# Weight parts of the first layer and of the experts at other distances from their activations, modulo 256 bytes

## The chip, the cores and the metric

One core of one Trainium2 chip runs the whole program. The time is that of the device, in microseconds; lower is better. The kernel before was timed at 2464.36 us, the median of two runs (2462.41 and 2466.32).

## The reference, cut to what matters

A two-layer transformer-like block (256 image tokens, 256 context tokens, width 1024) and then a second block on the image tokens, all in float32.

```python
for layer in range(2):
    p_lat = h_lat @ w_in[layer]            # q, kv, hyena v/x/y, gates
    ...                                    # attention and a long convolution
    mix = (g_attn * (o_attn @ w_br_attn) + g_hy * (o_hy @ w_br_hy)) @ w_out
    x = x + g1 * mix
    if layer == 0: x = x + g2 * swiglu(h)  # dense feed-forward, 2816 hidden; the context tokens too
    else:          x = x + g2 * moe_swiglu(h)   # 8 experts of 2816 hidden, the two best of each token
x = rmsnorm(x, final_g)
# second block: feed-forward, mixer, feed-forward, each between norms
```

Nearly all of the time is matrix products with weights that are read once: 574 MB come from HBM.

## The kernel before, in words

**One weight tile.** Weights lie in HBM as tiles of 128 partitions by up to 1024 columns. `wraw` (line 525) loads one by DMA from the SP queue into a buffer `raw`. `whl` (line 540) splits it into two parts of type fp32r whose sum is the weight: ScalarE copies it rounded to `whi` (`split`, line 502), VectorE writes the rest to `wlo`. `mm3` (line 497) then makes each product from three matmuls, weight high by activation high, weight high by activation low, weight low by activation high, and the line of all matmuls in the profile is that of the helper `mm`, L495. A tile of eight 128-column chunks so gives 24 matmuls. Every matmul loads its own stationary operand of 128 columns, and the load for the next matmul runs beside the present one.

**Who is stationary.** In layer 0, layer 1 and block 2 the weight chunk is stationary and the activations move: 512 columns (image and context tokens together) in layer 0 and for keys and values, 256 in layer 1 and block 2. In the experts (`moe`) and for `v2` the activations (`xe`, `hm`, `h`) are stationary and the weights move, 512 columns at a time, 256 in the last of an expert's six groups of hidden columns (`g == 5`) and for `v2`.

**Where tiles lie.** Tiles come from pools, each a stretch of bytes in every partition, laid out one behind another: first `w` (four `whi` and four `wlo`), then `r` (four `raw`); in the first two layers `b1` (13 general tiles of 8192 bytes: `h`, `fh`, `mg`, `o`, `oh`) and `k1` (work tiles); in the experts `r2`, `k2`, `t2`; in block 2 `b3` and `k3` behind the pool `x2` of the tiles `xsh` and `xsl`. Each `whi` and `wlo` is `self.wc` = 1024 columns of 4 bytes, so all start at a multiple of 256 bytes, and so do their chunks of 512 bytes. The activations of layers 0 and 1 (`h`, `fh`, `mg`, `o`, `oh`) and of the experts (`xe`, `hm`) start at multiples of 256 too. In block 2 the two tiles of `x2` are 8256 and 8320 bytes long (`XPAD` = 16 columns), together 192 more than a multiple of 256, so all of `b3` starts at 192.

In what follows the distance of a matmul is the address of the stationary operand that is loaded next, less the address of the moving operand, modulo 256 bytes. It is 0 in layer 0, in layer 1 and in the experts; it is 64 in block 2, where weights at 0 meet activations at 192, and 192 for `v2`, where the roles are swapped.

**Order.** The tile framework orders ScalarE, VectorE and TensorE by priority; SP and POOL run in program order. The order of the instructions does not follow from addresses.

**Normalisation.** `SumSq.rsqrt` (line 360) computes a reciprocal root with a Newton step. It uses a work tile `nm` (one buffer of `self.kn` columns: 512 in the first two layers and the experts, 256 in block 2), beside `nr`, and the squares lie in a ring of four buffers `a`.

Of the kernel before, what the change touches and what calls it, by code (L numbers as in the profile page):

```python
# [9 lines left out]
F32R = mybir.dt.float32r  # L10
# [315 lines left out]
class SumSq:  # L326
# [33 lines left out]
    def rsqrt(self, out=None):  # L360

        p, N, nf = self.p, self.N, self.nf
        if self.acc is not None:
            self.add(self.acc, True)
        n = self.ss.shape[1]
        m = p.wk("nm", n, 1)
        r = p.wk("nr", n, 1)
        p.act(r, self.ss, AF.Abs_reciprocal_sqrt, scale=1.0 / nf, bias=p.epsc if self.eps == EPS else p.eps2)
        p.stt(m, r, -0.5 / nf, r, OP.mult, OP.mult)
        p.stt(m, self.ss, self.eps * nf, m, OP.add, OP.mult)  # L370
        out = r if out is None else out
        p.stt(out, m, 1.5, r, OP.add, OP.mult)
        return out
# [91 lines left out]
class Prog:  # L465
# [53 lines left out]
    def ring(self, name, n, dt, i):  # L519
# [2 lines left out]
        pool = self.rp2 if k >= 4 else self.wp if i else self.rp  # L522
        return pool.tile([128, n], dt, name=name, tag=f"{name}{k}", bufs=1)

    def wraw(self, key, c=slice(None)):
        src = self.wsrc(key)[0][:, c]
        n = src.shape[1]
        raw = self.ring("raw", 1024, F32, 0)
        self.dma(raw[:, :n], src)
        return raw[:, :n]  # L530
# [4 lines left out]

    def w(self, key, k, **kw):

        return self.whl(self.wraw(key), k, **kw)

    def whl(self, raw, k, bufs=None, beside=False):  # L540
        n = raw.shape[1]
        c = n // k
        per = max(1, min(k, self.wc // c))
        r = []
        for s in range(0, k, per):
            m = min(per, k - s)
            if bufs:
                hi, lo = bufs[0]
                bufs.append(bufs.pop(0))
            else:  # L550
                hi, lo = self.ring("whi", self.wc, F32R, 1), self.ring("wlo", self.wc, F32R, 2)
                self.wpairs = (self.wpairs + [(hi, lo)])[-4:]
            with ExitStack() as es:
                es.enter_context(self.tc.high_priority(offset=self.early))
                for ins in self.hold:
                    es.enter_context(self.tc.issue_after(ins))
                if beside:
                    self.act(hi[:, :n], raw)
                    h3, r3 = (t[:, :n].rearrange("p (k c) -> p k c", c=128) for t in (hi, raw))
                    self.tt(h3[:, :, 96:], r3[:, :, 96:], h3[:, :, 64:96].bitcast(F32), OP.subtract)  # L560
                else:
                    self.split(hi[:, :m * c], lo[:, :m * c], raw[:, s * c:(s + m) * c])
            r += [(hi[:, i * c:(i + 1) * c], lo[:, i * c:(i + 1) * c]) for i in range(m)]
        return r
# [84 lines left out]
    def build(self):  # L649
        nc, tc = self.nc, self.tc  # L650
        with ExitStack() as es:
            es.enter_context(tc.manual_schedule(engines={SP, POOL}))
            self.cp = es.enter_context(tc.tile_pool(name="cp", bufs=1))
            self.ps = es.enter_context(tc.tile_pool(name="ps", bufs=1, space=PSUM))
            self.dp = es.enter_context(tc.tile_pool(name="dp", bufs=1, space=DRAM))
            cp = self.cp
            self.cv = cp.tile([128, CTOTAL], F32, name="cv")
            self.ident = cp.tile([128, 128], F32, name="ident")
            self.ones = cp.tile([128, 128], F32, name="ones")

            few = cp.tile([128, 8], F32, name="few")
            self.epsc, self.eps2, self.small, self.tneg = (few[:, i:j] for i, j in ((0, 1), (1, 2), (2, 3), (3, 5)))
            self.gp = cp.tile([128, 6, 8], F32, name="gp")
            self.sp = cp.tile([128, 8], F32, name="sp")
            self.mod = [cp.tile([128, 2, 48], F32, name=f"mod{l}") for l in range(2)]
            self.ada = cp.tile([128, 72], F32, name="ada")
            self.gn = cp.tile([128, 16, 8], F32, name="gn")
            self.xt = cp.tile([128, 8, 512], F32, name="xt")
            self.x = [self.xt[:, k, :] for k in range(8)]
            self.xl = [self.xt[:, k, :NT] for k in range(8)]  # L670
            self.kspill = [self.dp.tile([128, 2048], F32, name=f"ksp{l}") for l in range(2)]
            self.route = cp.tile([128, 10], F32, name="router")
            self.frn = cp.tile([128, 2, 8], F32, name="frn")

            self.rs = cp.tile([128, 8, 2, 8], F32, name="route")
            self.cnt = cp.tile([1, 1], I32, name="cnt")
            self.spill = [self.dp.tile([128, 2048], F32, name=f"sp{i}") for i in range(3)]
            nc.vector.memset(self.ones, 1.0)
            nc.vector.memset(self.epsc, EPS)
            self.fga = cp.tile([128, 2, 8], F32, name="fga")  # L680
            nc.vector.memset(self.eps2, EPS * EPS)
            nc.vector.memset(self.small, 1e-26)
            self.kn, self.early = 512, EARLY[0]
            self.wc, self.turn, self.wbufs, self.wpairs = 1024, [0, 0, 0], [4, 4, 4], []
            self.hold = ()
            c1 = es.enter_context(tc.tile_pool(name="c1", bufs=1))
            self.rope = c1.tile([128, 2, NT], F32, name="rope")
            self.mcst = c1.tile([128, 128 + 256 + 64 + 64], F32, name="mcst")
            with ExitStack() as s0:
                self.wp, self.rp = (s0.enter_context(tc.tile_pool(name=n, bufs=1)) for n in ("w", "r"))  # L690
                with ExitStack() as s1:
                    self.bp = s1.enter_context(tc.tile_pool(name="b1", bufs=13))
                    self.kp = s1.enter_context(tc.tile_pool(name="k1", bufs=1))
                    self.startup()
                    self.layer0()
                    self.layer1()
                self.xsp = s0.enter_context(tc.tile_pool(name="x2", bufs=1, reuse_waits="tile"))
                self.latter("")

            with tc.If(self.most > 128), ExitStack() as s0:  # L700
                self.wp, self.rp, self.xsp = (s0.enter_context(tc.tile_pool(name=n, bufs=1)) for n in ("wg", "rg", "xg"))
                self.latter("g")
# [717 lines left out]
    def moe(self, tp, general):  # L1420
        nc, kp, tc = self.nc, self.kp, self.tc
        m = self.mod[1]
        x = self.xl
# [12 lines left out]
        raws, lows = [], []  # L1436

        def fetch():
            if order:
                key, s, k = order.pop(0)  # L1440
                raws.append((self.wraw(key, s), k))

        def use(key, s, k):
            return ready.pop(0)
# [1 line left out]
        def used():  # L1446

            if raws:
                with self.tc.high_priority(offset=0 if order or len(raws) > 4 else -LATER2):
                    ready.append(self.whl(*raws.pop(0)))  # L1450
                lows.append(self.lo_ins)
                fetch()
        for _ in range(MRAW - 1):
# [162 lines left out]
        def again():  # L1616

            raw = kp.tile([128, 4, 1024], F32, name="xraw", tag="xe", bufs=2)
            turn, bufs = [0], [(self.ring("whi", 1024, F32R, 1), self.ring("wlo", 1024, F32R, 2)) for _ in range(4)]

            def use2(key, s, k):
                turn[0] = (turn[0] + 1) % 4
                t = raw[:, turn[0], :]
                self.dma(t, self.wsrc(key)[0][:, s])
                return self.whl(t, k, bufs)
            self.dma(self.xt[:, :, :NT], self.spill[0].rearrange("p (a b) -> p a b", a=8))
            for i in range(2):
                self.dma(raw[:, 2 * i:2 * i + 2, :], self.spill[1 + i].rearrange("p (a b) -> p a b", a=2))
                self.act(ht[i], raw[:, 2 * i:2 * i + 2, :])
            S = xe = None  # L1630
            for base in (128, 0):
                for e in range(NE):
                    if e % 2 == 0:
                        S = onehot(base, e // 2, S)
                        ST = weights(e // 2, S)
                        xe = gather(e // 2, S, xe)
                    y = expert(e, xe, use2, lambda: None)
                    if base or e < 7:
                        scatter(e, y, ST)
            return (7, y, ST), lambda: [use2((nm, 1, i), slice(0, 1024), 8) for i in range(2) for nm in "gu"]  # L1640
# [342 lines left out]
```

## Time and profile before

| | us |
|---|---|
| median of the two runs | 2464.36 |
| the profiled execution, as timed | 2460.6 |
| its span, first to last instruction | 2458.1 |
| TensorE busy in it | 2400.1 |
| VectorE busy | 1991.8 |
| ScalarE busy | 1500.0 |
| mean granted TensorE clock, share of the full 2.4 GHz | 0.990 |

The profile is of one execution. PE is TensorE's matmuls, PEld its loads of stationary operands, which overlap the matmuls; DVE is VectorE, ACT ScalarE. The bars of matmuls overlap one another, so PE is busy even where a matmul could start sooner. Addresses are not in the trace; the distances above follow from the layout of the pools.

### The profile page before, as it was taken

What the parts mean: (1) busy time and instruction counts of PE and PEld (TensorE: products, weight loads), DVE (VectorE), ACT (ScalarE), POOL (GpSimd) and SP (SyncE); (2) the same over time, 40 slices, a digit from 0 to 9 for tenths busy, and PEclk for the clock granted to TensorE, in tenths of its full rate; (3) what the DMA queues carried; (4) which work ended last, traced back from release to release, by engine and by line L of the source; (5) the groups of instructions that cost most, each with busy time, mean ns of one, the idle gap of its engine ahead of it and who ended that gap; (6) DMA issues with size and microseconds to landing.
All of it is one profiled execution on the core that took longest, in us unless ns stands there. A gap on an engine that the chain in (4) does not pass through costs nothing. (4 is left out here: it accounts for less than half of the span.)

```text
span 2458.1 us, 37467 instructions
## 1 busy us (share of the span) xinstructions
PE 2400.1 (98%) x13896; PEld 2054.5 (84%) x13896; DVE 1991.8 (81%) x3001; ACT 1500.0 (61%) x2214; POOL 89.6 (4%) x170
## 2 busy tenths in 40 slices
PE   8999999999999899999999999999999999999997
PEld 4677887788888698988888888888889998998997
DVE  6787799896878877789988998998987578977655
ACT  6676324422224676687777777777776558767544
POOL 0000011211121000000000000000000000000000
PEclk9999999999999999999999999999999999999999
DMA  7122365687886243699999999999984563454553
GB/s 287 49 92 88 137 230 223 236 293 271 281 312 223 83 140 126 205 382 350 343 351 353 352 339 365 352 332 355 357 298 152 191 220 121 155 176 164 192 194 113
DMA packets 161247, 582.71 MB, mean 237 GB/s; under 512 B 18000, under 2 KB 19536, under 8 KB 159904
## 3 DMA queue, kind: packets, MB, share of 16 engines
q1 hardware_dynamic: 136912, 491.35, 56.1%
q0 software_dynamic: 23600, 88.35, 9.8%
q8 instruction: 111, 1.82, 0.3%
q14 instruction: 80, 0.66, 0.1%
q10 hardware_dynamic: 544, 0.52, 0.1%
HBM read 573.87 MB, written 6.29 MB: 236 GB/s over the span
## 5 line engine op out<-in xcount | busy, mean ns | idle before, releaser
L481 ACT ACTIVATE whi<-raw 128x1024 fp32r<-128x1024 f32 (+1 forms) x902 | 918.2, 1046 | 600.1 <-PE acc L495 376.7
L484 DVE TENSOR_TENSOR wlo<-raw,whi 128x1024 fp32r<-128x1024 f32 (+1 forms) x900 | 1063.8, 1207 | 231.3 <-ACT whi L481 223.2
L495 PE MATMUL acc<-h,whi 128*128 128x256 f32 (+1 forms) x3648 | 829.4, 321 | 9.6 <-ACT h L481 4.6
L495 PEld LDWEIGHTS acc<-h,whi 128*128 128x128 f32 x3648 | 606.2, 189 | 68.2 <-ACT h L481 6.3
L495 PE MATMUL acc<-h,wlo 128*128 128x256 f32 (+1 forms) x1808 | 577.6, 320 | 1.1 <-DVE wlo L484 1.1
L495 PE MATMUL acc<-whi,xe 128*128 128x512 f32 (+1 forms) x1536 | 451.0, 373 | 0.3 <-ACT whi L481 0.3
L495 PEld LDWEIGHTS acc<-h,wlo 128*128 128x128 f32 x1808 | 342.1, 189 | 26.8 <-DVE wlo L484 1.5
L495 PEld LDWEIGHTS acc<-whi,xe 128*128 128x128 f32 x1536 | 280.9, 189 | 48.2 <-ACT whi L481 0.8
L495 PE MATMUL acc<-wlo,xe 128*128 128x512 f32 (+1 forms) x768 | 289.3, 377 | 0.2
L492 DVE SCALAR_TENSOR_TENSOR junk<-wt,rows 128x1024 bf16<-128x1024 f32 x200 | 238.8, 1220 | 4.2 <-DMA wt<-in_w 3.1
L495 PE MATMUL acc<-fh,whi 128*128 128x256 f32 (+1 forms) x1056 | 230.3, 315 | 0.7 <-DVE fh L484 0.6
L495 PE MATMUL y<-whi,hm 128*128 128x512 f32 x704 | 228.5, 395 | 0.0
L495 PEld LDWEIGHTS acc<-fh,whi 128*128 128x128 f32 x1056 | 172.5, 188 | 15.2 <-DVE fh L484 1.5
L495 PEld LDWEIGHTS acc<-wlo,xe 128*128 128x128 f32 x768 | 144.7, 188 | 30.5 <-DVE wlo L484 6.1
L495 PE MATMUL acc<-fh,wlo 128*128 128x256 f32 (+1 forms) x528 | 165.6, 314 | 0.5 <-DVE wlo L484 0.5
L495 PEld LDWEIGHTS y<-whi,hm 128*128 128x128 f32 x704 | 131.3, 188 | 27.4 <-ACT hm L481 3.1
L495 PE MATMUL y<-wlo,hm 128*128 128x512 f32 x352 | 138.5, 397 | 0.6
L495 PEld LDWEIGHTS acc<-fh,wlo 128*128 128x128 f32 x528 | 99.2, 188 | 7.6 <-DVE wlo L484 0.7
L636 POOL DMA_DIRECT2D wt<-in_w x152 | 81.4, 540 | 343.8 <-DVE junk L492 300.0
L495 PE MATMUL acc<-mg,whi 128*128 128x256 f32 (+1 forms) x384 | 86.7, 319 | 0.9 <-DVE mg L484 0.9
L495 PEld LDWEIGHTS y<-wlo,hm 128*128 128x128 f32 x352 | 66.1, 188 | 18.4 <-DVE wlo L484 3.6
L481 ACT ACTIVATE hm<-tp 128x512 fp32r<-128x512 f32 (+1 forms) x48 | 26.9, 561 | 75.0 <-PE tp L1561 74.9
(373 smaller groups left out, 2746.7 us busy)
## 6 DMA issues: line engine op xcount, KB each, us to landing
raw<-in_w SPq DMA_DIRECT2D x890, 512.0 KB, 5.5
wt<-in_w POOLq DMA_DIRECT2D x152, 512.0 KB, 5.7
raw<-in_w SPq DMA_DIRECT2D x24, 384.0 KB, 3.1
xt<-in_x SPq DMA_DIRECT2D x4, 512.0 KB, 9.8
ksp<-hf POOLq DMA_DIRECT2D x2, 1024.0 KB, 5.5
kf<-ksp SPq DMA_DIRECT2D x2, 1024.0 KB, 5.1
sp<-ht POOLq DMA_DIRECT2D x2, 1024.0 KB, 10.3
raw<-in_w SPq DMA_DIRECT2D x8, 256.0 KB, 2.7
```

What stands on the lines that cost most here:

```text
L481: return self.nc.scalar.activation(out, in_, func, **kw)
L484: return self.nc.vector.tensor_tensor(out, a, b, op=op)
L492: return self.nc.vector.scalar_tensor_tensor(out, a, s, b, op0=op0, op1=op1, **kw)
L495: return self.nc.tensor.matmul(out, lhsT=lhsT, rhs=rhs, start=start, stop=stop)
L636: self.nc.gpsimd.dma_start(t[:, i, :], self.wsrc(key)[0])
```

## The change

`whi` and `wlo` become 64 columns (256 bytes) wider, and a weight part is written `off` columns into its tile. `shift(key)` says how far by the kind of the weight:

- layer 1's `q`, `v`, `x`, `y`, `ga`, `gh`, `br`, `wo`, `ukq`: 16 columns, distance 64;
- layer 0's `q`, `v`, `x`, `y`, `ga`, `gh`, `br`, `wo`, `kv`: 40 columns, distance 160;
- layer 0's feed-forward `g`, `u`, `d`: 24 columns, distance 96;
- the experts' gate and up `mg`, `mu`: 32 columns, distance 128 (the weights move here), and 48 in the last group, distance 64;
- the experts' down `md`: 8 columns, distance 224;
- block 2's `v2`: 32 columns, distance 64;
- all others (block 2's other weights, `uv`, `rope`, layer 0's `ukq`, layer 1's `kv`): 0, as before.

The 2048 bytes that the eight wider tiles take are found by `rsqrt`, which takes one of the `a` buffers in place of `nm` where `self.kn` is 512. The list `wpairs`, which nothing read, goes.

```diff
--- before.py
+++ after.py
@@ -363,7 +363,7 @@
         if self.acc is not None:
             self.add(self.acc, True)
         n = self.ss.shape[1]
-        m = p.wk("nm", n, 1)
+        m = p.wk("a", n, 4) if p.kn == 512 else p.wk("nm", n, 1)
         r = p.wk("nr", n, 1)
         p.act(r, self.ss, AF.Abs_reciprocal_sqrt, scale=1.0 / nf, bias=p.epsc if self.eps == EPS else p.eps2)
         p.stt(m, r, -0.5 / nf, r, OP.mult, OP.mult)
@@ -522,6 +522,21 @@
         pool = self.rp2 if k >= 4 else self.wp if i else self.rp
         return pool.tile([128, n], dt, name=name, tag=f"{name}{k}", bufs=1)
 
+    def shift(self, key):
+
+
+        if key[0] in ("q", "v", "x", "y", "ga", "gh", "br", "wo", "ukq") and key[1] == 1:
+            return 16
+        if key[0] in ("mg", "mu"):
+            return 48 if key[2] == 5 else 32
+        if key[0] == "md":
+            return 8
+        if key[0] in ("q", "v", "x", "y", "ga", "gh", "br", "wo", "kv") and key[1] == 0:
+            return 40
+        if key[0] in ("g", "u", "d") and key[1] == 0:
+            return 24
+        return 32 if key[0] == "v2" else 0
+
     def wraw(self, key, c=slice(None)):
         src = self.wsrc(key)[0][:, c]
         n = src.shape[1]
@@ -535,9 +550,9 @@
 
     def w(self, key, k, **kw):
 
-        return self.whl(self.wraw(key), k, **kw)
-
-    def whl(self, raw, k, bufs=None, beside=False):
+        return self.whl(self.wraw(key), k, off=self.shift(key), **kw)
+
+    def whl(self, raw, k, bufs=None, beside=False, off=0):
         n = raw.shape[1]
         c = n // k
         per = max(1, min(k, self.wc // c))
@@ -548,8 +563,8 @@
                 hi, lo = bufs[0]
                 bufs.append(bufs.pop(0))
             else:
-                hi, lo = self.ring("whi", self.wc, F32R, 1), self.ring("wlo", self.wc, F32R, 2)
-                self.wpairs = (self.wpairs + [(hi, lo)])[-4:]
+                hi, lo = self.ring("whi", self.wc + 64, F32R, 1), self.ring("wlo", self.wc + 64, F32R, 2)
+                hi, lo = hi[:, off:off + self.wc], lo[:, off:off + self.wc]
             with ExitStack() as es:
                 es.enter_context(self.tc.high_priority(offset=self.early))
                 for ins in self.hold:
@@ -681,7 +696,7 @@
             nc.vector.memset(self.eps2, EPS * EPS)
             nc.vector.memset(self.small, 1e-26)
             self.kn, self.early = 512, EARLY[0]
-            self.wc, self.turn, self.wbufs, self.wpairs = 1024, [0, 0, 0], [4, 4, 4], []
+            self.wc, self.turn, self.wbufs = 1024, [0, 0, 0], [4, 4, 4]
             self.hold = ()
             c1 = es.enter_context(tc.tile_pool(name="c1", bufs=1))
             self.rope = c1.tile([128, 2, NT], F32, name="rope")
@@ -1438,7 +1453,7 @@
         def fetch():
             if order:
                 key, s, k = order.pop(0)
-                raws.append((self.wraw(key, s), k))
+                raws.append((self.wraw(key, s), k, self.shift(key)))
 
         def use(key, s, k):
             return ready.pop(0)
@@ -1447,7 +1462,8 @@
 
             if raws:
                 with self.tc.high_priority(offset=0 if order or len(raws) > 4 else -LATER2):
-                    ready.append(self.whl(*raws.pop(0)))
+                    raw, k, off = raws.pop(0)
+                    ready.append(self.whl(raw, k, off=off))
                 lows.append(self.lo_ins)
                 fetch()
         for _ in range(MRAW - 1):
@@ -1616,7 +1632,7 @@
         def again():
 
             raw = kp.tile([128, 4, 1024], F32, name="xraw", tag="xe", bufs=2)
-            turn, bufs = [0], [(self.ring("whi", 1024, F32R, 1), self.ring("wlo", 1024, F32R, 2)) for _ in range(4)]
+            turn, bufs = [0], [[self.ring(nm, 1088, F32R, i)[:, :1024] for nm, i in (("whi", 1), ("wlo", 2))] for _ in range(4)]
 
             def use2(key, s, k):
                 turn[0] = (turn[0] + 1) % 4
```

## Rows read from the trace of the kernel before

**Rows 1.** The page's part 1: busy us (share of the span) and instructions

```profile
PE 2400.1 (98%) x13896; PEld 2054.5 (84%) x13896; DVE 1991.8 (81%) x3001; ACT 1500.0 (61%) x2214; POOL 89.6 (4%) x170
```

**Rows 2.** Windows by stage: length, busy us (count) by engine (page's order), clock, DMA

```profile
500.00:810.00 310.00, 305.29 (x1343) 251.56 (x1341) 248.16 (x394) 93.10 (x121) 54.09 (x101) 1.00 0.75 271
810.00:1035.00 225.00, 216.24 (x1574) 200.72 (x1575) 177.37 (x336) 150.33 (x275) 0.00 (x0) 0.98 0.41 135
1050.00:1830.00 780.00, 778.37 (x3767) 642.07 (x3766) 706.70 (x741) 594.06 (x672) 0.00 (x0) 1.00 0.95 352
```

**Rows 3.** Windows without a gap: stretch, length, PE busy (bars caught), clock, DMA

```profile
600.00:620.00 20.00, 20.00 (x90) 1.00 0.71 246
986.00:1006.00 20.00, 20.00 (x169) 1.00 0.61 180
2320.00:2340.00 20.00, 20.00 (x179) 1.00 0.57 185
```

**Rows 4.** Tile h, layer 0's feed-forward: count, bar ns min/median/max, first and last start

```profile
L495 PE MATMUL acc<-h,whi x182: 389/389/389, 599.8 to 661.2; 128*128 128x512 f32 x182
L495 PEld LDWEIGHTS acc<-h,whi x181: 187/188/188, 599.8 to 661.0; 128*128 128x128 f32 x181
```

**Rows 5.** Tile h, layer 1, 860 to 975 us, same view

```profile
L495 PE MATMUL acc<-h,whi x399: 274/283/386, 859.8 to 973.5; 128*128 128x256 f32 x200
L495 PEld LDWEIGHTS acc<-h,whi x398: 186/192/193, 859.9 to 973.4; 128*128 128x128 f32 x199
```

**Rows 6.** Tile h, block 2's second feed-forward, 2230 to 2300 us, same view

```profile
L495 PE MATMUL acc<-h,whi x158: 276/276/384, 2273.0 to 2299.9; 128*128 128x256 f32 x158
L495 PEld LDWEIGHTS acc<-h,whi x158: 186/188/192, 2272.9 to 2299.8; 128*128 128x128 f32 x158
```

**Rows 7.** Tile h, block 2's mixer, 2040 to 2140 us; third row v2

```profile
L495 PE MATMUL acc<-h,whi x360: 276/281/387, 2055.0 to 2139.8; 128*128 128x256 f32 x180
L495 PEld LDWEIGHTS acc<-h,whi x361: 186/188/192, 2054.8 to 2140.0; 128*128 128x128 f32 x181
L495 PE MATMUL acc<-whi,h x64: 276/279/283, 2067.5 to 2105.9; 128*128 128x256 f32 x64
```

**Rows 8.** Timeline, layer 0: start, us, engine, line, what, count, idle before

```profile
101.35 0.39 PE L495 MATMUL acc<-h,wlo 128*128 128x512 f32 x1
102.03 0.19 PEld L495 LDWEIGHTS sc<-kt,gq 96*128 96x128 f32 x1 [0.72 <-ACT gq L481]
```

**Rows 9.** Groups by line, 101.6 to 101.9 us: count, busy us, mean ns

```profile
L495 PE MATMUL acc<-h,wlo 128*128 128x512 f32 x1 | 0.4, 388 | 0.0
```

**Rows 10.** Same view, 202.95 to 203.04 us, the only TensorE group there

```profile
L495 PE MATMUL acc<-h,whi 128*128 128x512 f32 x1 | 0.4, 397 | 0.0
```

**Rows 11.** Same view, the experts, 1050 to 1830 us

```profile
L495 PE MATMUL acc<-whi,xe 128*128 128x512 f32 x1280 | 403.7, 391 | 0.3 <-ACT whi L481 0.3
L495 PE MATMUL acc<-wlo,xe 128*128 128x512 f32 x640 | 253.1, 395 | 0.2
L495 PE MATMUL y<-whi,hm 128*128 128x512 f32 x689 | 223.7, 395 | 0.0
L495 PE MATMUL y<-wlo,hm 128*128 128x512 f32 x344 | 135.3, 396 | 0.6
L495 PE MATMUL acc<-whi,xe 128*128 128x256 f32 x256 | 47.3, 283 | 0.0
```

**Rows 12.** Same view, layer 0, 0 to 810 us

```profile
L495 PE MATMUL acc<-h,whi 128*128 128x512 f32 x1248 | 393.1, 393 | 1.1 <-ACT whi L481 1.1
L495 PE MATMUL acc<-h,wlo 128*128 128x512 f32 x616 | 241.7, 392 | 0.0
```

**Rows 13.** Tile views of h (1840:2020 us) and xe (1100:1800): DVE's writes

```profile
L492 DVE SCALAR_TENSOR_TENSOR h<-xa,ada,h x8: 476/479/482, 1853.3 to 1860.7; 128x256 fp32r<-128x256 f32 x8
L492 DVE SCALAR_TENSOR_TENSOR xe<-tp,mod,xe x24: 475/478/487, 1205.2 to 1611.8; 128x256 fp32r<-128x256 f32 x24
```

**Rows 14.** Tile nm, whole span

```profile
L492 DVE SCALAR_TENSOR_TENSOR nm<-nr x15: 160/426/693, 37.1 to 2446.2; 128x256 f32<-128x256 f32 x8, 128x512 f32<-128x512 f32 x6, 128x2 f32<-128x2 f32 x1
```

## The prediction, made before the changed kernel was run

> **What bounds the kernel now.** I read the first part of the page first: TensorE has a matmul in flight for 2400.1 us, 98% of the span [rows 1]. The windows by stage say the same of each place that the change touches: 305.29 of 310 us in layer 0's feed-forward part, 216.24 of 225 in layer 1, 778.37 of 780 in the experts, where DVE (706.70) and the DMA engines (share 0.95, 352 GB/s) are near full too [rows 2]. So the end is set by how fast matmuls follow one another, and a weight part that is ready sooner is worth nothing. A change of placement can pay only through the length of a matmul.
>
> Next I read that length. Bars of matmuls overlap, so a bar is longer than the distance from one start to the next. A window without a gap catches (window + bar) / distance bars, and solving that for three windows of 20 us [rows 3] with the bars of the same places [rows 4 to 6] gives (20000 + 389) / 90 = 226.5 ns for 512 columns in layer 0, (20000 + 283) / 169 = 120.0 for 256 columns in layer 1, and (20000 + 276) / 179 = 113.3 for 256 columns in block 2. A bar is thus some 163 ns longer than the distance of starts, and I read a change of one as the same change of the other. The reader is to see two things. Layer 1 and block 2 run the same 128x256 fp32r matmuls at the full granted clock, yet one takes 6.7 ns longer, and its weight loads last 192 ns instead of 188 [rows 5, 6]. By the placement told above, what differs is the distance modulo 256 bytes: 0 in layer 1, 64 in block 2. And the 512-wide matmuls, at distance 0 too, have weight loads of 188 ns, the undisturbed length [rows 4].
>
> **The change part by part.**
> *256-wide matmuls.* Shifts of 16 (layer 1), 48 (last expert group) and 32 (v2) columns bring all three to block 2's distance, stationary operand 64 bytes beyond the moving one. In layer 1 the tiles of q (3), v, x, y (12), gates (16), br (8) and wo (8) are 47 of 24 matmuls, 1128, and the query halves of ukq add 54: 1182. They take 283 ns now [rows 5]. At distance 64 block 2 shows 276 in its feed-forward part [rows 6], but 281 in its mixer [rows 7]. Bounds: 2 to 7 ns each, 2.4 to 8.3 us. Layer 1 is a mixer, yet its longest unbroken stretch (br) streams like a feed-forward [rows 3], so I take 5 ns: 5.9 us. Last expert group: 8 experts x 2 matrices x 24 = 384 matmuls at 283 [rows 11], same bounds, 0.8 to 2.7 us; I take 4 ns, 1.5 us. v2: 96 matmuls at 279 now (distance 192) [rows 7], to 276 or 281; I take 3 ns, 0.3 us. Together 7.7 us.
>
> *512-wide matmuls.* Layer 0 gets distance 160 (49 tiles x 24 = 1176 matmuls) and 96 (gate and up 44 x 24 = 1056, down 528); the experts 128 (gate and up, 1920) and 224 (down, 1056). That is 5736 matmuls of 226.7 ns, more than half of the span: one ns on each is 5.7 us, and this is the term that decides. No row has a 512-wide fp32r matmul followed by an fp32r load at these distances. What there is: the load beside them is not stretched [rows 4], and a matmul beside which nothing was loaded (start 101.35, next load 102.03 [rows 8]) has a bar of 388 [rows 9] against 389 with a load beside it [rows 4]. So the load costs such a matmul about 1 ns now; a better distance can save that and no more: 0 to 5.7 us. The other bound is the slow bar, 397 [rows 10], against 389: +8 ns or +45.9 us. Between them I take 0, nearest to rows 4 and 9. The cover that makes it 0 is the stream: in a 256-wide sequence load after load fits into 113.3 ns, so a 512-wide matmul leaves the next load some 113 ns of slack, and a stretched load costs only what exceeds that.
>
> *The slow bars.* In the experts the 512-wide means are 391, 395, 395 and 396 [rows 11]: over 389 that is 1280 x 2 + 640 x 6 + 689 x 6 + 344 x 7 ns = 12.9 us. In layer 0 they are 393 and 392 [rows 12]: 1248 x 4 + 616 x 3 ns = 6.8 us, part of it start-up and late data. Could the distance be their cause? The bar of 397 had no load beside it at all [rows 10], so mostly not. I take a fifth of the 19.7 us, 4 us; bounds 0 and 19.7.
>
> *The rest.* ACT and DVE write the parts 32 to 192 bytes further into a tile. DVE's 128x256 op took 479 ns into a tile at 192 modulo 256 and 478 into one at 0 [rows 13], so 0; if it were dearer, the experts would feel it first, where DVE has 73 us left [rows 2]. The "nm" tile becomes one of the four "a" buffers in up to 15 normalisations whose ops last at most 693 ns [rows 14]. The buffer it takes was handed out four "a" tiles earlier, so I expect no wait, 0; at worst each waits for one such op, 15 x 0.69 = 10 us. The tiles' 256 bytes more move later pools by whole multiples of 256, 0. DMAs, the queues and the counts of instructions stay.
>
> *Sum.* 5.9 + 1.5 + 0.3 + 0 + 4 = 11.7 us off the profiled run: 2460.6 to 2448.9. That run is 3.8 us below the median of 2464.4, so against the median 2452.7; I say 2453.
>
> **The rivals.**
> *No effect.* What separates layer 1 from block 2 may be the company (what ACT and DVE do beside it), not the distance. For it: block 2's mixer at distance 64 shows 281 too. Against it: loads of 192 stand where the distance is 0, and 188 in both parts of block 2 [rows 5 to 7]. It gives 2464. The Trainium skill ("TensorE: Matmul & The Clock Gate", section "Part 2: What happens when you issue a matmul") speaks for it: TensorE has two independent read ports, and loading the next weights "doesn't steal SBUF read bandwidth from the running matmul". By that rule every gain above is zero and the time stays 2464. The trace agrees with it at 512 columns (388 against 389) and not at 256 (120.0 against 113.3).
>
> *The 512-wide ones pay too.* If distance 0 costs every matmul the 6.7 ns that it costs a 256-wide one, and the four distances free them, 5736 x 6.7 = 38.4 us go beside the 7.7: 2464.4 - 46.1 = 2418. The experts' 2976 x 6.7 = 19.9 us of 780 ask the DMA for 361 GB/s instead of 352 [rows 2], a small step. For it: every 512-wide row stands at distance 0, so none shows what another would give. Against it: rows 4 and 9, and 226.5 is twice 113.3, as if both widths streamed at one rate. The Trainium skill (same page, section "Back-to-back issue gap") gives N/2.4 + 2.5 ns for a warm matmul, 215.8 at 512 columns; by it 5736 x 10.9 = 62.5 us could go beside the 7.7, to 2394, as an estimate. No row here shows a 512-wide fp32r matmul that short.
>
> *Slower.* The 512-wide ones stand well at 0, and the new distances put the load's reads across the stream's, as 0 does at 256 columns. Place: layer 0 and the experts. Price: 4 ns each (halfway to the bar of 397) is 22.9 us, 2480 after the 7.7; 8 ns is 45.9 us, 2503. It decides from 7.7 us / 5736 = 1.3 ns a matmul on. For it: at 256 columns only 64 shows 276; 0 shows 283 and 192 shows 279 [rows 5 to 7]. Against it: the 113 ns of slack.
>
> **How the numbers follow.** Forecast 0.57 (its own range 2445 to 2461, from the small bounds above), no effect 0.12, the 512-wide ones pay too 0.15, slower 0.16. The likeliest gives 2453. For 8 in 10 I reach down to 2420 (leaving out 0.11, most of the third) and up to 2482 (4.4 ns a matmul; leaving out 0.09). A change of 2% is about what a measurement of this kernel can tell from none: 2415 and 2514. Below 2415 needs 7.3 ns off each 512-wide matmul: 0.10. Above 2514 needs 9.9 ns on each, more than the slowest bar: 0.03. Within: 0.87.
>
> **What would show it.** Right: layer 1's bars at 276 to 281 and its loads at 188; the last expert group below 281; layer 0's feed-forward still at 389; the experts' means within 2 ns of now. The 512-wide ones pay too: bars near 382 in layer 0's feed-forward and more matmuls per 20 us there. Slower: loads of 192 beside 512-wide matmuls, bars of 393 to 397 throughout. No effect: layer 1 still at 283 and 192. Wrong above all if the feed-forward bars of layer 0, all 389 now, move at all: nothing but the distance changes there.

## The result, and the profile after

The changed kernel took 2490.44 us, the median of two runs (2490.19 and 2490.70), against 2464.36: a ratio of 1.0109 with a 95% interval of 1.0092 to 1.0126. I had forecast 2453, 11 us less; it became 26 us more, and 8 us beyond the upper end of my range. What came is the rival that I had called slower.

The head of the profile page of the changed kernel:

```profile
span 2488.2 us, 37468 instructions
## 1 busy us (share of the span) xinstructions
PE 2423.8 (97%) x13896; PEld 2052.4 (82%) x13896; DVE 1994.8 (80%) x3001; ACT 1497.8 (60%) x2214; POOL 89.3 (4%) x170
```

The span is 30.1 us longer than in [rows 1]; PE is busy 23.7 us longer, DVE and ACT the same within 3 us. So it is TensorE that needs longer for the same matmuls. The windows by stage say where. I cut both traces at the same places of the program: start-up, layer 0 up to its feed-forward, that feed-forward, layer 1, the experts, block 2. First the kernel before (columns: window, its length, busy us and count of each engine, granted clock, DMA share, GB/s):

```profile
48.00:432.00 384.00, 378.89 (x1744) 297.18 (x1743) 318.02 (x576) 207.69 (x357) 19.92 (x37) 0.99 0.39 139
432.00:803.00 371.00, 370.95 (x1618) 301.78 (x1617) 305.24 (x490) 120.66 (x163) 67.52 (x126) 1.00 0.74 270
803.00:1049.00 246.00, 230.20 (x1644) 212.09 (x1643) 190.90 (x371) 161.34 (x296) 1.96 (x3) 0.97 0.43 143
1049.00:1836.00 787.00, 785.27 (x3797) 647.12 (x3797) 712.10 (x749) 597.01 (x677) 0.00 (x0) 1.00 0.95 351
1836.00:2458.00 622.00, 594.03 (x4937) 580.29 (x4935) 435.30 (x709) 384.21 (x669) 0.00 (x0) 0.98 0.50 166
```

and the same stages of the changed kernel:

```profile
48.00:440.00 392.00, 385.06 (x1742) 297.47 (x1743) 318.63 (x576) 207.58 (x357) 19.86 (x37) 0.99 0.38 136
440.00:823.00 383.00, 382.94 (x1617) 302.72 (x1616) 307.20 (x490) 119.83 (x164) 67.26 (x126) 1.00 0.73 262
823.00:1067.00 244.00, 225.81 (x1647) 207.21 (x1646) 191.04 (x371) 161.75 (x297) 1.96 (x3) 0.98 0.42 141
1067.00:1863.00 796.00, 794.47 (x3792) 647.89 (x3792) 712.61 (x747) 596.43 (x675) 0.00 (x0) 1.00 0.95 348
1863.00:2488.00 625.00, 594.55 (x4934) 580.86 (x4934) 434.74 (x708) 382.63 (x669) 0.00 (x0) 0.98 0.50 165
```

With counts within five and a clock within 0.01 of each other, layer 0 takes 8 + 12 us longer, the experts 9, block 2 3, and layer 1 takes 2 us less: together the 30 us. Layer 0 and the experts are where 512-wide matmuls stand.

The bars say the same. Layer 0's feed-forward in a window without a gap, and the instructions on `h` there (duration: least, median, most):

```profile
600.00:620.00 20.00, 20.00 (x87) 16.10 (x86) 15.42 (x26) 4.70 (x6) 4.27 (x8) 1.00 0.74 262
```

```profile
L495 PE MATMUL acc<-h,whi x218: 392/397/400, 599.9 to 676.0; 128*128 128x512 f32 x109
L495 PEld LDWEIGHTS acc<-h,whi x217: 187/188/192, 599.9 to 675.8; 128*128 128x128 f32 x109
```

Where 90 matmuls were caught [rows 3], 87 are now: (20000 + 396) / 87 = 234.4 ns from start to start instead of 226.5. Every bar is longer than the 389 of [rows 4], while the loads keep their median of 188. In what follows "from start to start" is the mean time between one start and the next that the trace records in a stretch, leaving out those more than 26 ns above the usual one, where something else came between. Over the whole feed-forward of layer 0 it went from 226.7 to 234.3, and 1583 x 7.6 ns = 12.0 us are that stage's 12.

The experts' groups by form, where [rows 11] had 391, 395, 395, 396 and twice 283:

```profile
L495 PE MATMUL acc<-whi,xe 128*128 128x512 f32 x1248 | 398.3, 395 | 0.9 <-DVE xe L492 0.7 <-ACT whi L481 0.2
L495 PE MATMUL acc<-wlo,xe 128*128 128x512 f32 x624 | 248.5, 398 | 0.1
L495 PE MATMUL y<-whi,hm 128*128 128x512 f32 x663 | 217.8, 399 | 0.0
L495 PE MATMUL y<-wlo,hm 128*128 128x512 f32 x332 | 131.7, 400 | 0.6 <-DVE wlo L484 0.2
L495 PE MATMUL acc<-whi,xe 128*128 128x256 f32 x224 | 39.9, 278 | 0.0
L495 PE MATMUL acc<-wlo,xe 128*128 128x256 f32 x112 | 31.4, 280 | 0.0
```

The 512-wide ones are 3 to 4 ns longer, the 256-wide ones 3 to 5 shorter. Layer 1, at distance 64 now, has a median of 281 where [rows 5] had 283, with many at 276:

```profile
L495 PE MATMUL acc<-h,whi x341: 276/281/375, 881.1 to 974.3; 128*128 128x256 f32 x171
```

Whether the longer bar needs a load beside the matmul, the bars of matmuls without one don't settle. In layer 0's mixer of the changed kernel this matmul (start 145.12) runs alone, since the next load starts at 145.58, and its bar is 389, although its weights are shifted like their neighbours', whose bar of 399 stands in the same view:

```profile
145.12 0.39 PE L495 MATMUL acc<-h,wlo 128*128 128x512 f32 x1
...
145.58 0.53 PEld L495 LDWEIGHTS sc<-kt,gq 96*128 96x128 f32 x3 [0.51 <-ACT gq L481]
```

```profile
L495 PE MATMUL acc<-h,whi 128*128 128x512 f32 x1 | 0.4, 399 | 0.0
L495 PE MATMUL acc<-h,wlo 128*128 128x512 f32 x1 | 0.4, 389 | 0.0
```

But another one (start 53.14, next load at 53.46) has a bar of 397:

```profile
53.14 0.40 PE L495 MATMUL acc<-h,wlo 128*128 128x512 f32 x1
53.46 0.29 PEld L495 LDWEIGHTS adac<-fold,a 2*128 2x128 f32 x2 [0.37 <-issue]
```

```profile
L495 PE MATMUL acc<-h,wlo 128*128 128x512 f32 x1 | 0.4, 397 | 0.0
```

Of the 51 such 512-wide matmuls in the changed kernel (no load beside them, the next start over 253 ns later, the bar under 420) 25 have a bar of 397 and 17 one of 388 or 389; of the 55 in the kernel before, without any shift, it is 29 and 24. So a lone matmul can be as long without the shifts as with them.

### The profile page after: what moved, and what is told of

Read it like the earlier page. It is cut to its first block, busy times and chain, and to the rows that moved or that the text cites. A ratio compares the mean times of both kernels' runs of the same rounds, so it can differ in the third digit from the quotient of the medians.

```text
span 2488.2 us, 37468 instructions
## 1 busy us (share of the span) xinstructions
PE 2423.8 (97%) x13896; PEld 2052.4 (82%) x13896; DVE 1994.8 (80%) x3001; ACT 1497.8 (60%) x2214; POOL 89.3 (4%) x170
## 5 line engine op out<-in xcount | busy, mean ns | idle before, releaser
L495 PEld LDWEIGHTS acc<-wlo,xe 128*128 128x128 f32 x768 | 144.6, 188 | 30.1 <-DVE wlo L484 3.9
L484 DVE TENSOR_TENSOR a<-a,acc 128x256 f32<-128x256 f32 (+2 forms) x64 | 33.3, 520 | 51.0 <-PE acc L495 49.2
```

The costliest lines, as they stand in the source:

```text
L484: return self.nc.vector.tensor_tensor(out, a, b, op=op)
L495: return self.nc.tensor.matmul(out, lhsT=lhsT, rhs=rhs, start=start, stop=stop)
```

## The experiments

The theory: how fast 512-wide matmuls follow one another depends on the distance between the operand that streams and the one that is loaded beside it, 0 is the good one, and the change took all 5736 of them off it. The rivals: the wider tiles, the lent `a` buffer and the new order of the instructions cost the time; or it is the place of the weights by themselves, not the distance. Each diff is against the changed kernel unless it says otherwise, and `...` marks what is left out. Where a diff shows only new lines in `shift`, its old lines go.

**The 256-wide shifts alone.**

```diff
-        if key[0] in ("mg", "mu"):
-            return 48 if key[2] == 5 else 32
...
+        if key[0] in ("mg", "mu") and key[2] == 5:
+            return 48
...
```

> Keeps the change's shifts of layer 1, of the experts' last group and of v2 (256-wide matmuls, distance 64) and puts all 512-wide ones back to distance 0. Theory: the distance alone sets the cadence of a 512-wide matmul, and what the change lost it lost there. Then layer 0's feed-forward streams at 226.7 ns from start to start again (234.3 with the change), layer 1 keeps its 116.4 (119.7 before), and the time is 3 to 8 us under the kernel before: 2456 to 2461. Rival, the wider tiles, the lent a buffer and the new order of the instructions cost the time: it stays near the changed kernel, 2480 to 2490, with layer 0 near 234.

Measured: 2462.94 us, a ratio of 0.9999 (0.9987 to 1.001). Layer 0's feed-forward:

```profile
600.00:620.00 20.00, 20.00 (x90) 16.57 (x89) 14.21 (x22) 7.35 (x9) 3.21 (x6) 1.00 0.74 260
```

90 matmuls again, at 226.7 ns. Layer 1 keeps its gain: 116.1 ns from start to start (119.7 before), 201.5 us from its first matmul to its output projection (203.9). So the loss lies in the 512-wide shifts. But the 3 to 8 us of gain that I expected against the kernel before didn't come in the end.

**The 512-wide shifts alone.**

```diff
-        if key[0] in ("q", "v", "x", "y", "ga", "gh", "br", "wo", "ukq") and key[1] == 1:
-            return 16
...
-            return 48 if key[2] == 5 else 32
+            return 0 if key[2] == 5 else 32
...
-        return 32 if key[0] == "v2" else 0
+        return 0
```

> Keeps the shifts of the 512-wide matmuls alone (layer 0 at 160 and 96, experts at 128 and 224), everything 256-wide is back at its old distance. Theory: layer 0 and the experts lose what they lost with the change and layer 1 is back at 119.7 ns, so 3 to 8 us over the changed kernel: 2493 to 2499. Rival, the rearrangement of memory and order costs the time: as the changed kernel without its gains at 256 columns, which is 2493 to 2499 too, so the two are told apart by the other kernels of this call and not by this one; it gives the sum: if the parts add, this one's loss and the narrow one's gain make the change's 26 us.

Measured: 2492.61 us, 1.0125 (1.0105 to 1.0145), just under the expected 2493. Layer 0's feed-forward runs at 234.3 ns, layer 1 at 119.7. By this pair of kernels (2492.61 and 2490.44) the 256-wide gain is about 2 us, which their intervals don't tell from none.

**No shift at all.**

```diff
     def shift(self, key):
+        return 0
```

> The change with every shift at 0: tiles 64 columns wider, the lent a buffer, the new order of the instructions, distances as before. Theory (distance): 2464 within 4 us, layer 0's feed-forward at 226.7 ns from start to start, layer 1 at 119.7. Rival, memory and order cost the time: 2480 to 2500, with layer 0 near 234.

Measured: 2464.58 us, 1.0013 (0.9998 to 1.0027), 90 matmuls in the same window:

```profile
600.00:620.00 20.00, 20.00 (x90) 16.57 (x89) 14.20 (x22) 6.59 (x9) 2.81 (x6) 1.00 0.70 244
```

Wider tiles, lent buffer and new order together are worth 2 to 3 us, not 26, and the interval doesn't tell them from nothing. That rival falls. The 512-wide shifts alone cost 2492.61 - 2464.58 = 28.0 us against this kernel.

**Both sides moved by 96 bytes.**

```diff
     def shift(self, key):
+        return 0 if key[0] in ("mg", "mu", "md", "in2", "v2", "bo", "wo2") or key[0] in "gud" and key[1] else 24
...
+                    pad = s1.enter_context(tc.tile_pool(name="pad", bufs=1))
+                    pad.tile([128, 24], F32, name="pad")
                     self.bp = s1.enter_context(tc.tile_pool(name="b1", bufs=13))
```

> Weights of layers 0 and 1 shifted by 24 columns, and a tile of 96 bytes put ahead of the pool of the activations, so that both lie at 96 modulo 256 and the distance is 0 as in the kernel before, while each one's own place is the changed kernel's or a new one; experts and block 2's weights at 0. Theory (distance): layer 0's feed-forward at 226.7 ns from start to start with bars of 389, layer 1 at 119.7, 2460 to 2470. Rival (what counts is where the weights lie by themselves, 96 being a bad place): layer 0 stays at 234 ns as with the change, about 3300 matmuls by 6 to 7.6 ns, 2484 to 2490.

Measured: 2464.50 us, 1.0011 (0.9999 to 1.0023). Layer 0's feed-forward has its weights at 96 as in the changed kernel, and the bars of the kernel before:

```profile
L495 PE MATMUL acc<-h,whi x190: 389/389/389, 599.7 to 663.8; 128*128 128x512 f32 x190
```

So the place of the weights by itself does nothing; the distance does.

**Two sweeps of the distance.** In the first, in steps of 32 bytes:

```diff
     def shift(self, key):
+        if key[0] in ("mg", "mu", "md"):
+            return 8 * key[1]
+        if key[0] in ("g", "u") and key[1] < 2:
+            return 8 * (key[2] // 3)
+        if key[0] in ("ga", "gh", "br", "wo") and key[1] == 1:
+            return 8 * key[2]
+        return 0
```

> A sweep of the distance in steps of 32 bytes within one run. Expert e has its weights 8*e columns further (stationary less moving: -32*e modulo 256); layer 0's feed-forward gate and up weights go up by 8 columns every third group of hidden columns (distance 0, 32, ... 224), and so do those of block 2's first feed-forward (from 64 on); layer 1's ga, gh, br and wo by 8 columns for each of their eight tiles; all else at 0. Theory A (only distance 0 suits a 512-wide matmul, anything else makes it wait for a read of the load): 226.7 ns from start to start in expert 0 and in layer 0's first groups and 231 to 237 everywhere else. Theory B (the same distance suits both widths, and 64 is it): 226.7 at 64 also, with the disturbed matmuls of the experts gone there, and 120.0 at 0 against 113.3 at 64 for the 256-wide ones of block 2. Theory C (the cost goes smoothly with the distance, most at 128): lowest at 0, highest at 128, the same at 32 and 224. Against the kernel before, some 2 x 850 of the 1056 gate and up matmuls in layer 0 and 7/8 of 2592 in the experts lie off 0: by theory A about 2464 + (900 + 2270) x 6 ns = 2483.

In the second, each of these returns 4 columns more, and layer 0's `d` 64:

> The sweep again, 16 bytes further everywhere (distances 16, 48, ... 240; the experts at -32*e - 16), and layer 0's down weights 64 columns further, a whole 256 bytes. In the first sweep the mean from start to start at 512 columns was 227.7 at 0, 233.3 at 32 and 64, 234 at 96, 231 to 231.7 at 128, 233.3 at 160, 229 to 230 at 192, 233.3 at 224; at 256 columns 119.4 at 0, 118.2 at 32, 116.2 (114 to 116) at 64, 118.6 at 96, 119.5 at 128, 120 at 160, 117.7 at 192, 117 at 224. If the cost goes smoothly with the distance, the new ones lie between their neighbours: 228 to 233 at 16 and 240, 230 to 232 at 208; and at 256 columns none lies under 64. If a step of 32 bytes is what counts (a distance within one step behaves like its beginning), 16 is as 0 and 208 as 192. If neither, distances off a multiple of 32 cost more than both neighbours, 235 and more. The modulus: with a whole 256 bytes more, layer 0's down matmuls stay at 226.7; if a longer period counts (512 bytes), they leave it for 231 or more.

Measured: 2487.89 us and 2485.67 us (one run each). The means from start to start in ns, 47 to 144 matmuls for each entry of layer 0 (525 at 0), 338 to 349 for the experts, 41 to 144 for block 2 and 46 or 47 for the experts' last group; entries at multiples of 32 are from the first sweep, the others from the second (0: layer 0's down products and expert 0):

| distance | 512, layer 0 | 512, experts | 256, block 2 | 256, experts' last group |
|---|---|---|---|---|
| 0 | 226.8 | 227.6 | 120.0 | 119.9 |
| 16 | 233.3 | 235.7 | 120.0 | 117.2 |
| 32 | 233.3 | 233.0 | 118.3 | 118.4 |
| 48 | 233.3 | 234.1 | 117.9 | 119.2 |
| 64 | 233.4 | 233.3 | 115.1 | 114.1 |
| 80 | 232.0 | 232.4 | 119.0 | 119.2 |
| 96 | 234.2 | 234.0 | 118.2 | 118.6 |
| 112 | 233.3 | 232.8 | 119.9 | 115.8 |
| 128 | 232.4 | 232.5 | 119.5 | 118.7 |
| 144 | 233.3 | 230.9 | 118.8 | 113.3 |
| 160 | 233.4 | 233.2 | 119.9 | 120.0 |
| 176 | 230.1 | 231.0 | 118.1 | 118.4 |
| 192 | 229.0 | 230.1 | 117.8 | 117.8 |
| 208 | 231.8 | 232.3 | 116.7 | 118.3 |
| 224 | 233.4 | 233.2 | 117.0 | 116.8 |
| 240 | 228.3 | 231.3 | 118.2 | 113.5 |

The numbers that the expectation of the second sweep quotes from the first are too low in two places: its 231 to 231.7 at 128 leaves out matmuls that started 240 or 241 ns apart with nothing between them, and its 119.4 at 0 is 120.0. The changed kernel's own distances fit the table: 234.3 at 96, 233.4 at 160, 232.5 at 128, 233.2 at 224.

Two stretches of layer 0 in the first sweep, at distance 0 and then at 32:

```profile
L495 PE MATMUL acc<-h,whi x89: 389/389/395, 451.9 to 481.8; 128*128 128x512 f32 x89
```

```profile
L495 PE MATMUL acc<-h,whi x87: 395/396/396, 484.8 to 514.9; 128*128 128x512 f32 x87
```

Six nanoseconds lie between neighbours of one run and one stage, which in the kernel before streams at 226.7 throughout. Theory A holds in the main: at 512 columns 0 is the best of 16 distances, in both places, and every other one costs 1.5 to 8 ns, though in layer 0 176, 192 and 240 cost less than the 231 that it gave as the least. It isn't smooth (theory C: 128 costs no more than 32 or 96, and 16 costs as much as 96), a step of 32 bytes isn't what counts either (16 is not like 0), and distances off a multiple of 32 don't cost 235 and more throughout. Theory B falls too: 64 helps the 256-wide matmuls and costs the 512-wide ones 6 ns. A period of 256 fits: with 64 columns more, layer 0's down products keep their bars (the second sweep; 226.8 from start to start):

```profile
L495 PE MATMUL acc<-fh,whi x224: 389/389/397, 672.5 to 814.6; 128*128 128x512 f32 x112
```

At 256 columns the experts' last group doesn't follow block 2 (113.3 against 118.8 at 144), so there the distance isn't all; I come back to it at the end.

**The lent buffer alone**, against the kernel before:

```diff
-        m = p.wk("nm", n, 1)
+        m = p.wk("a", n, 4) if p.kn == 512 else p.wk("nm", n, 1)
```

> The kernel before with one edit of the change: the root's Newton step takes one of the four a buffers in place of nm; tiles as wide as before, no shift. In the kernel with every shift at 0 the stretch from layer 0's first projection to its output projection is 3.3 us longer than before (337.6 against 334.3). If the lent buffer makes a normalisation wait there, it is 337 here too and the time 2464 to 2468; if the wider tiles (another order of the instructions) do it, it is 334 and the time is that of the kernel before within 2 us.

Measured: 2464.62 us, 1.0016 (1.0001 to 1.0031), and 337.2 us in that stretch. TensorE, VectorE and ScalarE run their instructions in the same order here as in the changed kernel and the four kernels before the sweeps; the kernel before differs from them in 198 of TensorE's 13896 places, all in its first 114 us. So the new order comes with the lent buffer, and the wider tiles add nothing to either (2464.58 and 2464.62 us, 337.6 and 337.2). The lent buffer, with the order that it brings, is where the narrow kernel's gain went, as far as it can be told: some 2 us are at the edge of these intervals.

**Two attempts at a version that beats both.** The first, in part, against the kernel with the 256-wide shifts alone:

```diff
-        m = p.wk("a", n, 4) if p.kn == 512 else p.wk("nm", n, 1)
+        m = p.wk("nm", n, 1)
...
-            return 48
-        return 32 if key[0] == "v2" else 0
+            return 4
+        return 0
...
-                hi, lo = self.ring("whi", self.wc + 64, F32R, 1), self.ring("wlo", self.wc + 64, F32R, 2)
+                hi, lo = self.ring("whi", self.wc + 16, F32R, 1), self.ring("wlo", self.wc + 16, F32R, 2)
...
-            self.rs = cp.tile([128, 8, 2, 8], F32, name="route")
+            self.rs = self.gn.rearrange("p (a b) e -> p a b e", b=2)
```

> An attempt at a version that beats both: tiles only 16 columns wider, paid for by letting the experts' small routing tile use the bytes of the layers' gain tile (done with by then), so that the root keeps its own nm tile; layer 1 shifted by 16 columns (distance 64), the experts' last group by 4 (distance 240, 113.5 ns from start to start in the second sweep against 119.2 at 0), v2 and all 512-wide matmuls as in the kernel before. If the lent buffer cost what the narrow kernel gained: layer 1 shorter by 2.4 us (201.5 against 203.9), the last groups by 384 x 3 to 5.7 ns = 1 to 2 us, layer 0 as before, 2458 to 2460 and a ratio of 0.998 to 0.9985. If the new order of instructions or the choice of another buffer moves more than that: within 3 us of the kernel before to either side.

Measured: 2490.56 us, 1.0112 (1.0094 to 1.0131). I had overlooked that tiles of 1040 columns begin 64 bytes further each, so the eight buffers have eight places and the distances of 0, 64, 128 and 192 follow one another. Layer 0's bars show it:

```profile
L495 PE MATMUL acc<-h,whi x201: 387/392/404, 599.7 to 669.1; 128*128 128x512 f32 x101
L495 PE MATMUL acc<-h,wlo x101: 389/397/398, 599.9 to 669.4; 128*128 128x512 f32 x101
```

A mistake, and once more the theory: 512-wide matmuls at 231 to 232 ns with none of the change's shifts on them, and block 2, which no shift touches, at 118.1 in place of the 114.4 to 115.4 of the others (the sweeps apart).

The second, in part, keeps every tile at a multiple of 256 bytes, with the 256-wide shifts of the first experiment:

```diff
+    def part(self, i, n):
+        wide = i == 1 or (self.turn[2] + 1) % self.wbufs[2] < 3
+        t = self.ring(("whi", "wlo")[i - 1], self.wc + 64 * wide, F32R, i)
+        return t[:, n * wide:n * wide + self.wc]
...
-            h = self.feat = self.kp.tile([128, 256], F32, name="feat")
+            h = self.feat = self.mcst[:, z * 256:z * 256 + 256]
```

> The attempt once more without the mistake of the kernel with tiles 16 columns wider (its tiles began 64 bytes further each, so that distances of 0, 64, 128 and 192 were mixed everywhere). Seven of the eight tiles are 64 columns wider, the last wlo is not and stays at 0, so every tile begins at a multiple of 256 bytes; the 1792 bytes come from the experts' routing tile laid over the gain tile, from the small feature tile laid over the bytes of later constants, and from 256 spare ones; the root keeps nm. Shifts as in the narrow kernel (layer 1: 16 columns, last expert group: 48, v2: 32), 512-wide all at 0. If the lent buffer is what held back the narrow kernel: layer 0 to its output projection in 334 to 335 us, layer 1 in 201.5 to 202, 2458 to 2461, a ratio of 0.998 to 0.999. If it is the new order of the instructions that costs 2 to 3 us: 337 there and a ratio of 0.9995 to 1.001.

Measured: 2458.34 us, a ratio of 0.999 (0.9974 to 1.0006): 1% under the changed kernel, and not to be told from the kernel before. Layer 0's stretch took 336.0 us, layer 1 203.8 (no gain, although with one buffer in eight unshifted its matmuls came at 117.2 ns from start to start). My expectation of both stretches was missed, so that the total lies where I had put it is no support. That the stretch is 336 with `nm` kept leaves open what in the new orders costs these 2 us.

## Why the prediction was wrong

**The 512-wide matmuls: here it failed.** I took this term at 0 between bounds of 1 ns gained and 8 ns lost. It was 7.6 ns from start to start in layer 0's feed-forward (12 us), 5.2 ns in its projections (228.0 to 233.2; 5 to 6 us of that stage's 8, the rest is the order's), and 4.1 ns in the experts (228.6 to 232.7; 12 us, of which the stage's 9 remain after the gain of the last groups and less time lost between matmuls). By the times of whole kernels it is 28.0 us over 5736 matmuls, 4.9 ns each, inside the bounds but far from the end that I chose.

The choice rested on two readings. The first, 388 without a load beside and 389 with one [rows 4, 9], compared with a single lone matmul, and [rows 10] had another of 397; such bars come out both ways in the kernel before and in the changed one, so they don't tell what a load costs. All those rows stood at distance 0, too, and 389 was the shortest bar in them that came again and again: from a good place one can only go to a worse one. I used them as if they bounded every distance. The second, that 113 ns of slack behind the load hide whatever happens to it, looked at the wrong victim. The load isn't stretched (188 in the median), it is the streaming matmul that is: 392 to 400 where it had 389. No slack behind the load helps a matmul that is itself late, in a stage where TensorE never rests. The one pair of rows that showed the effect, 120.0 and 113.3 at 256 columns [rows 3], showed a longer matmul too; I had put it down to the load's 192.

**The 256-wide ones: right in sign, smaller in the end.** I said 7.7 us. Layer 1 and its output projection went from 119.7 and 119.5 to 116.5 and 114.7 (-2.5 us of their stages, 5.9 forecast), the last expert group from 119.7 to 115.0 (384 x 4.7 = 1.8 us, 1.5 forecast), v2 from 117.6 to 115.2 (0.2). The times of whole kernels put the sum at about 2 us (2464.58 to 2462.94, and 2492.61 to 2490.44), within their intervals. Most of layer 1 didn't stream like the feed-forward that I chose but like block 2's mixer [rows 7], the other end of my bounds.

**The slow bars: wrong.** I gave 4 us to a freeing of them. At the new distances no 512-wide mean fell, and at distance 0 they stay as they were (391, 396, 395 and 396 in the kernel with the 256-wide shifts alone, against [rows 11]). The trace of the kernel before shows what they are. The means of [rows 11] hold 86 bars of over 440 ns, 8 us of the excess over 389, nearly all of them first matmuls after something else; and most of the others come soon after such a break, before the stream settles. Layer 0's feed-forward begins so (443.9 to 445.2 us), and then stays at 389 (445.6 to 530):

```profile
L495 PE MATMUL acc<-h,whi x4: 393/396/499, 444.0 to 445.0; 128*128 128x512 f32 x4
...
L495 PE MATMUL acc<-h,whi x249: 389/389/389, 445.5 to 529.8; 128*128 128x512 f32 x125
```

In the experts the second matmul after a break (another kind of matmul, or a start over 26 ns late) has a bar of 396 in the mean, the tenth one of 389. In the changed kernel they don't settle: 394 and 395 there.

**The rest: nearly right.** DVE and ACT are as busy as before, DMA moves as much. The lent buffer, which I had at 0 with 10 at worst, costs about 2 us by its own run, with the order that it brings.

**The rivals.** "Slower" had place and price right: layer 0 and the experts, 4 ns a matmul, 2480; 4.9 ns and 2490 came. Of its two signs the bars came and the loads of 192 did not (188 in the median). I gave it 0.16 for the slack's sake. "The 512-wide ones pay too" has the wrong sign. "No effect" fell, and these runs speak against the rule that went with it (the Trainium skill, "TensorE: Matmul & The Clock Gate", section "Part 2: What happens when you issue a matmul"): matmuls with the same loads beside them follow one another 7.6 ns later at 96 than at 0. That it is the load's read that delays them is argued from the distance being that between the two operands; no run takes the loads away. Nor did any distance bring the 512-wide matmuls under 226.7 ns in the mean, so the 215.8 worked out from the formula of the same page's section "Back-to-back issue gap", which the page gives for an isolated matmul, was not reached.

**What I said would show it** was well chosen: the feed-forward bars of layer 0 moved, and that was the sign that I had named for being wrong above all.

## What to carry to other kernels

Where every matmul has a weight load beside it, as here, the distance modulo 256 bytes between the two operands is a property of the layout with a price of several ns per matmul, and what is good differs with the width: here 0 was the best at 512 columns and among the worst at 256, where 64 was better by 5 ns. A run or two with the distance swept show it. A row without a loss at the present setting bounds what a change can gain there, not what it can lose. And tiles whose width is not a multiple of 256 bytes scatter the distances of the tiles behind them.

## What the runs showed of the hardware

- Once settled, 512-wide matmuls with a load beside each follow one another every 226.7 ns at distance 0, again and again; at 96 the time goes round in a pattern of seven, 232, 237, 238, 230, 235, 235, 233 ns (layer 0's feed-forward of the changed kernel, from 601.8 us on), 234.3 in the mean. The loads last 188 in the median in both.
- At 256 columns the distance alone doesn't settle the pace. Block 2 stands at 64 in all of the changed kernel, and streams there in two manners, each steady over tens of us:

```profile
1950.00:1970.00 20.00, 20.00 (x173) 20.00 (x172) 11.37 (x15) 9.62 (x15) 0.00 (x0) 1.00 0.63 187
2020.00:2040.00 20.00, 20.00 (x179) 20.00 (x178) 11.28 (x15) 9.79 (x15) 0.00 (x0) 1.00 0.57 179
```

```profile
L495 PE MATMUL acc<-h,whi x115: 281/281/281, 1949.8 to 1970.0; 128*128 128x256 f32 x115
L495 PEld LDWEIGHTS acc<-h,whi x115: 187/192/192, 1949.8 to 1970.0; 128*128 128x128 f32 x115
...
L495 PE MATMUL acc<-h,whi x119: 276/276/276, 2019.9 to 2040.0; 128*128 128x256 f32 x119
L495 PEld LDWEIGHTS acc<-h,whi x119: 187/188/188, 2019.9 to 2040.0; 128*128 128x128 f32 x119
```

173 and 179 matmuls in 20 us, 117.8 and 113.3 ns. Which of the two a stretch falls into changes between kernels that are the same there: block 2's first feed-forward ran at 113.4 to 116.3 ns in the mean, the sweeps and the kernel with scattered tiles apart. Block 2's 3 us in the table of stages are of this kind: from the last of the experts' down products to the last matmul it took between 607 and 613 us in the same kernels. What decides it is open.
- What the load and the stream share that has a period of 256 bytes, and whether it is the load that the stream waits for, these runs don't show.
